# Sums of the FFN output's weights: when they are asked for, which slots they use, and no low parts kept in DRAM

## The chip, the cores and the metric

The kernel runs on one core of a Trainium2 chip. The metric is the time of one execution in microseconds of the device. Before the change the median of three runs is 929.23 us (925.81 to 930.81).

## The reference

One layer of a decoder trunk on 512 tokens of width 1024, all float32. The stages that matter here:

```python
xn = _rmsnorm(h, norm1_w)
proj = xn @ w_in
z, xbc, dt_raw, q, k, v, qi, ki, wi, u, gates = _split_proj(proj)
...
y = _ssd_scan(xh, dt, A, Bm, Cm)                      # state-space mixer, chunks of 128 tokens
y_ssd = _rmsnorm((y + d_skip * xh) * jax.nn.silu(z), ssd_norm_w)
...
merged = g[:, :, 0] * (y_ssd @ w_up_ssd) + g[:, :, 1] * (y_att @ w_up_attn) + g[:, :, 2] * (y_pool @ w_up_pool)
h = h + merged @ w_out
hn = _rmsnorm(h, norm2_w)
a_part, b_part = jnp.split(hn @ w_ffn_in, 2, axis=-1)
return h + (jax.nn.silu(a_part) * b_part) @ w_ffn_out   # followed by one more RMSNorm
```

`w_ffn_out` has 2816 rows (the hidden units) and 1024 columns. It is an input, so sums of its parts can be formed at any time before the last product.

## The kernel before

**Number format.** TensorE multiplies float32 through pairs: each operand is split into a high part (`wh`, a cast to a shorter format by ACT) and a low part (`wl`, the difference, by DVE), and a product is three matmuls, high by high, high by low and low by high. `split` and `split_w` write these pairs for weights and activations; `raw` is a weight tile as loaded.

**Order of the stages on TensorE.** Its instructions stay in the order in which the program writes them (`manual_schedule` for PE). First come the index scores, keys, queries and values and the pooling projections; then, in `gate_merge(2, ...)`, the gates and the up projection of the pooling branch, then the channels of the convolution (`xbc`, twelve tiles) and the gate `z`; then `gate_merge(1, ...)` for attention and `gate_merge(0, ...)` for the state-space branch. `gate_merge` runs a loop over `f`: `gate(f)` loads gate weights and multiplies, `up(f)` multiplies the branch's output by its up projection and merges. For branches 1 and 2, `up` lags `gate` by two steps; for branch 0 all eight gates come first (`f` 0 to 7) and the eight up products after (`f` 8 to 15). Then follow the output projection (`token_major`, PE tile `acc`), the FFN's first product (tile `r`, seven block products per unit in a Strassen scheme) and its second (tile `o`, again seven products over a scheme of 2 by 2 blocks).

**The state-space chain.** `ssd_gens` is a stream: a generator whose steps `tick` puts between matmuls of whatever stage is running, by a clock that the program keeps while it is being written. After attention it builds, for each of two groups of heads, `btok`, `cbt` and four `xdt` (six slots of tag "A") and `selp` and three `hst` (four slots of "T2"); eight pairs of heads then each need DVE and ACT to make the decay matrix `L` (`seg` on PE, a minimum on DVE, exponentials on ACT, a product with `cbt` on DVE), then PE tiles `ebc`, `yd` and `yo`. Last, `ssd_norm` takes the mean square (`ssq`), its root (`rt`, two steps on DVE and one on ACT), spreads it (`rstd`), and splits the result into `ysh` (tag "yP") and `ysl` (eight slots of "A"), which the up products of branch 0 read. The chain runs beside the gates and up products of branch 1.

**The other engines.** Instructions of DVE, ACT, POOL and SP are not held to the program's order: they are put in order ahead of time by what is ready and has a slot, earlier program text first among ready ones. On the chip each engine then takes its own list strictly in order. SBUF tiles come from tags with a fixed number of slots (`SLOTS`: "A" 12, "T2" 8, "xbc" 12, "T1" 4 and so on); a tile waits until a slot of its tag is free.

**The sums.** For the second FFN product four of the seven right-hand sides are sums of blocks of `w_ffn_out`: U1 to U4. `prestage(u)` (u = 0 to 10, 11 units) loads four blocks `wb` (tag "T2", 256 KB each, by SP, L721), adds them on DVE into four `wsum` tiles (tag "xbc"), and for the two blocks that are used unsummed (products 1 and 2) makes high parts `whigh` on ACT and low parts `wlow` on DVE, all in "xbc". POOL's queue stores the four sums and two low parts in DRAM (L732; tensors U and L). The call stands in branch 0's loop: unit `f - 1` ahead of `gate(f)` for f = 1 to 11.

**The output stage.** `OUT` lists 42 steps (p, v): product p = 1, 2, 6, 5, 7, 4, 3, six steps each, the last of a product half as large. `prepare_out(n)` runs two steps ahead: it loads the right-hand side `oraw` (a block of `w_ffn_out`, or a stored sum; L1324), casts it to `wh` on ACT, and gets its low part `wl`: for products 1 and 2 by a load of L (L1337), else by a subtraction on DVE. `sums_left` makes sums of the hidden activations on DVE (`hid`, `xsum`) in products 1 and 2, and `split_left` splits the left-hand side (`hl`). Where nearly all operations go through a helper, the profile puts them on line 90, so groups are told apart by their tiles.

Of the kernel before, what the change touches and what calls it, by code (L numbers as in the profile page):

```python
# [8 lines left out]
F32 = mybir.dt.float32  # L9
R32 = mybir.dt.float32r  # L10
# [3 lines left out]
P = 128  # L14
# [81 lines left out]
def kernel(  # L96
# [91 lines left out]
    def nm(s):  # L188
        uid[0] += 1
        return f"{s}_{uid[0]}"  # L190
# [4 lines left out]
    def slot(tag, name, dtype=F32, shape=(P, T)):  # L195
        return spool.tile(list(shape), dtype, name=nm(name), tag=tag, bufs=SLOTS[tag])
# [514 lines left out]
    def stored(name, v):  # L711
        if (name, v) not in kept:
            kept[name, v] = sums_pool.tile([P, len(members(v)), T], F32, name=f"{name}_{v}", tag=f"{name}_{v}")
        return kept[name, v]

    def prestage(u):
        b = {}
        for c in range(2):
            for n in range(2):
                b[c, n] = slot("T2", "wb")  # L720
                SP.dma_start(b[c, n], wfo[c, n][:, u, :])  # L721
        got = {}
        for name, x, y in (("U1", b[0, 0], b[0, 1]), ("U2", "U1", b[1, 1]), ("U3", b[0, 1], b[1, 1]), ("U4", "U2", b[1, 0])):
            got[name] = slot("xbc", "wsum")
            DVE.tensor_tensor(got[name], got.get(x) if isinstance(x, str) else x, y, op=OP.add)
        for name, c in (("L1", 0), ("L2", 1)):
            h = slot("xbc", "whigh", R32)
            ACT.copy(h, b[c, 0])
            got[name] = slot("xbc", "wlow")
            DVE.tensor_tensor(got[name], b[c, 0], h, op=OP.subtract)  # L730
        for name, t_ in got.items():
            nc.gpsimd.dma_start(stored(name, u // 2)[:, u % 2, :], t_)  # L732

    def gate_merge(br, w_up, nk, yh, yl, ready):
        wd = 2048 // nk
        ths, raws = {}, {}

        def gate(f):
            if f % 2 == 0:
                raws["g"] = load_cols([(win, G0 + br * D + f * P, 256)], KD)  # L740

            def evac(ps):
                if br == 0:
                    if f % 4 == 0:
                        ths[f // 4, "all"] = slot("yA", "gths", F32, (P, 4, T))
                    ths[f] = ths[f // 4, "all"][:, f % 4, :]
                else:
                    ths[f] = slot("th", "gth")
                ACT.activation(ths[f], ps, AF.Tanh, scale=0.5)

            proj_job(raws["g"][:, :, tsl(f % 2)], evac)

        def up(f):
            if (f * P) % wd == 0:
                raws["u"] = load_cols([(w_up[0], f * P, wd)], nk)
            o = (f * P) % wd

            def body(w):
                ready()
                pu = pmm("up")  # L760
                product(pu, *w, yh, yl, nk)
                th = ths[f]
                if merged[f] is None:
                    merged[f] = slot("m", "merged")
                    DVE.scalar_tensor_tensor(merged[f], th, 1.0, pu, OP.add, OP.mult)
                else:
                    DVE.scalar_tensor_tensor(th, th, 1.0, pu, OP.add, OP.mult)
                    if br == 0:
                        DVE.tensor_tensor(merged[f], merged[f], th, op=OP.add)
                        finish_merged(f)  # L770
                    else:
                        POOL.tensor_tensor(merged[f], merged[f], th, op=OP.add)

            job(lambda: split_w(raws["u"][:, :, o:o + P], (P, nk, P)), body)

        skew = SKEW if br else KD
        for f in range(KD + skew):
            if br == 0 and 1 <= f <= NU:
                prestage(f - 1)
            if f < KD:  # L780
                gate(f)
            if f >= skew:
                up(f - skew)

    def mixes_ready():
        for st in mixes:
# [226 lines left out]
            st.live[0][1] = at + NLAG  # L1013
        return st

    def token_major(w, nk, ah, al, tail, done, ahead=None, tag=None):
        acc = {}
        for t in range(NT):
            for hf in range(2):
                acc[t, hf] = pmm("acc") if t < 2 else paux("acc")  # L1020
        keep = []

        def term(t, k, wh, wl, hfs=(0, 1)):
            a, b = ah(k)[:, tsl(t)], al(k)[:, tsl(t)]
            for hf in hfs:
                cs = slice(hf * T, hf * T + T)
                PE.matmul(acc[t, hf], lhsT=a, rhs=wh[:, cs], start=(k == 0), stop=False)
                PE.matmul(acc[t, hf], lhsT=a, rhs=wl[:, cs], start=False, stop=False)
            for hf in hfs:
                cs = slice(hf * T, hf * T + T)  # L1030
                PE.matmul(acc[t, hf], lhsT=b, rhs=wh[:, cs], start=False, stop=(k == nk - 1))
            tick()

        for k in range(nk):
            if k % 2 == 0:
                raw = (slot(tag, "raw", F32, (P, 2, D)) if tag else
                       wpool.tile([P, 2, D], F32, name=nm("raw"), tag="raw", bufs=2))
                SP.dma_start(raw, w[k * P:(k + 2) * P, :].rearrange("(k p) n -> p k n", p=P))
            wh, wl = split_w(raw[:, k % 2, :], (P, D))
            if k < nk - tail:  # L1040
                for t in range(NT):
                    term(t, k, wh, wl)
            else:
                keep.append((k, wh, wl))
        if ahead is not None:
            ahead()
        for t in range(NT):
            if t < NT - 1:
                for k, wh, wl in keep:
                    term(t, k, wh, wl)  # L1050
            else:
                for hf in range(2):
                    for k, wh, wl in keep:
                        term(t, k, wh, wl, (hf,))
            done(t, acc[t, 0], acc[t, 1])
# [271 lines left out]
    def prepare_out(n):  # L1327
        if n >= len(OUT):
            return
        p, v = OUT[n]  # L1330
        w = len(members(v))
        load_right(p, v)
        h = wpool.tile([P, 2, T], R32, name=nm("wh"), tag="wh")
        l = wpool.tile([P, 2, T], R32, name=nm("wl"), tag="wl")
        ACT.copy(h[:, :w, :], oraws[p, v])
        if p in (1, 2):
            SP.dma_start(l[:, :w, :].bitcast(F32), stored(f"L{p}", v))  # L1337
        else:
            DVE.tensor_tensor(l[:, :w, :], oraws[p, v], h[:, :w, :], op=OP.subtract)
        orights[p, v] = h, l  # L1340
        split_left(p, v)
        if n + 1 < len(OUT):
            load_right(*OUT[n + 1])
# [62 lines left out]
    def close_row(t):  # L1406
# [3 lines left out]
        DVE.tensor_scalar(ys[t][:, 1, :], ys[t][:, 1, :], rs, None, OP.mult)  # L1410
        SP.dma_start(of[tsl(t), T:D], ys[t][:, 1, :])

    prepare_out(0)
    prepare_out(1)
    for n, (p, v) in enumerate(OUT):
# [58 lines left out]
```

## Time and profile before

| what | us |
|---|---|
| median of three runs | 929.23 (925.81 to 930.81) |
| the profiled execution, its own time | 924.42 |
| its span, first to last instruction | 922.7 |
| TensorE busy | 886.4 (96%) |
| VectorE busy | 683.7 (74%) |
| ScalarE busy | 458.7 (50%) |
| GpSimd busy | 144.4 (16%) |
| mean granted clock of TensorE | 0.988 |

In rows of instructions each has its line, engine, operation, `out<-in` by tile names, shape and count. In a row of waits, "A x <- B y: total, times, longest" says that engine A sat idle before its instruction on tile x until B's on y ended; "DMA U<-wsum" as the releaser is the landing of a store of a sum, which also sets its slot free. A line of the order of time starts with its start and duration, and has in brackets the idle time before it and what ended that. In the tables by stretches each engine has its busy time and, in brackets, its count of instructions; PEclk is the clock granted to TensorE, 1.00 being full speed; the last two are the busy share and the rate of the DMA engines.

### The profile page before, as it was taken

The page shows a single profiled execution, that of the slowest core. Times are in us where ns is not written, and L with a number is a line of the kernel's source. Part 1 is how long each engine was busy: PE and PEld are TensorE (multiplying, and loading weights), DVE is VectorE, ACT ScalarE, POOL GpSimd, SP SyncE. Part 2 cuts the span into 40 slices and gives each one's busy share as a digit, 9 for nine tenths or more (in the row PEclk, how much of TensorE's full clock was granted, in tenths as well). Part 3 has the DMA queues.
Part 4 walks back from the last instruction along what each step waited for, and adds up shares of the span by engine and source line. Part 5 has one row for each costly group of instructions (what it writes and reads, how often), then busy time and mean ns, then how long its engine had stood idle before and what let it go on. Part 6 is the DMA issues. An engine that isn't in the chain of part 4 may idle for free.

```text
span 922.7 us, 13363 instructions
## 1 busy us (share of the span) xinstructions
PE 886.4 (96%) x5083; PEld 765.4 (83%) x5083; DVE 683.7 (74%) x1095; ACT 458.7 (50%) x791; POOL 144.4 (16%) x165
## 2 busy tenths in 40 slices
PE   9999999999999999887998999999999999999997
PEld 7877778888888777666786887999999999977885
DVE  5588999955654467777876635999888879766786
ACT  6546433355553244453542325965455455556665
POOL 3160000001110223446542002200000000001011
PEclk9999999999999999998999999999999999999998
DMA  7222112323212112757799725123422223697553
GB/s 242 69 92 92 46 46 92 94 89 92 92 47 81 57 46 92 233 189 248 256 408 363 264 92 182 47 92 130 145 92 92 93 98 108 220 340 249 183 193 127
DMA packets 95202, 134.10 MB, mean 145 GB/s; under 512 B 6745, under 2 KB 65697, under 8 KB 95138
## 3 DMA queue, kind: packets, MB, share of 16 engines
q1 hardware_dynamic: 88178, 113.58, 37.5%
q0 software_dynamic: 5280, 17.31, 4.7%
q10 hardware_dynamic: 1680, 2.36, 0.7%
q8 instruction: 40, 0.66, 0.3%
q14 instruction: 24, 0.20, 0.1%
HBM read 111.73 MB, written 21.50 MB: 144 GB/s over the span
## 4 chain that ended last, share of the span: by engine, by line
PE 38%; DVE 6%; DMA 5%; issue 3%; ACT 2%; POOL 1%; DVEq 0%; SPq 0%; POOLq 0%; ACTq 0%
PE r L90 23%; PE o L90 9%; PE up L90 4%; DMA wb<-in_w_ffn_out_dram 4%; PE acc L90 2%; DVE wl L90 2%; DVE ms L90 1%; DVE xr L90 1%; DMA wl<-L 1%; DMA U<-wsum 1%; DMA raw<-in_w_ffn_in_dram 1%; DVE wsum L90 1%; DVE wlow L90 0%; DVE early L90 0%; ACT acc L90 0%
## 5 line engine op out<-in xcount | busy, mean ns | idle before, releaser
L90 ACT CAST wh<-raw 128x1024 fp32r<-128x1024 f32 (+1 forms) x151 | 150.9, 1003 | 174.4 <-PE r L90 59.4
L90 DVE TENSOR_TENSOR wl<-raw,wh 128x1024 fp32r<-128x1024 f32 (+1 forms) x149 | 175.4, 1178 | 70.8 <-ACT wh L90 70.5
L90 PE MATMUL mm<-xnh,wh 128*128 128x512 f32 (+1 forms) x480 | 192.7, 402 | 0.0
L90 PE MATMUL mm<-xnh,wl 128*128 128x512 f32 (+1 forms) x480 | 183.4, 382 | 1.3 <-DVE wl L90 1.3
L90 PE MATMUL mm<-xnl,wh 128*128 128x512 f32 (+1 forms) x480 | 183.2, 382 | 0.3 <-DVE xnl L90 0.3
L90 PE MATMUL r<-T,wh 128*128 128x256 f32 x704 | 127.9, 283 | 0.0
L90 PEld LDWEIGHTS r<-T,wh 128*128 128x128 f32 x704 | 109.8, 192 | 0.0
L90 PEld LDWEIGHTS mm<-xnh,wl 128*128 128x128 f32 x480 | 90.5, 189 | 19.6 <-DVE wl L90 1.7
L90 PEld LDWEIGHTS mm<-xnh,wh 128*128 128x128 f32 x480 | 91.1, 190 | 15.9 <-issue 2.0
L90 PEld LDWEIGHTS mm<-xnl,wh 128*128 128x128 f32 x480 | 90.9, 189 | 15.5 <-issue 1.4
L90 PE MATMUL r<-T,wl 128*128 128x256 f32 x352 | 99.6, 283 | 0.0
L90 PE MATMUL o<-wh,hl 128*128 128x512 f32 x308 | 95.4, 390 | 0.1
L90 PE MATMUL r<-B,wh 128*128 128x256 f32 x464 | 84.8, 283 | 0.0
L90 PEld LDWEIGHTS r<-B,wh 128*128 128x128 f32 x464 | 72.4, 192 | 0.0
L90 PEld LDWEIGHTS o<-wh,hl 128*128 128x128 f32 x308 | 57.8, 188 | 12.3 <-ACT wh L90 0.5
L90 PEld LDWEIGHTS r<-T,wl 128*128 128x128 f32 x352 | 67.6, 192 | 0.0
L90 PE MATMUL r<-B,wl 128*128 128x256 f32 x232 | 65.7, 283 | 0.0
L90 PE MATMUL o<-wl,hl 128*128 128x512 f32 x154 | 60.6, 394 | 3.2 <-DVE wl L90 1.9
L90 POOL TENSOR_TENSOR ys<-xr,fnrow 128x512 f32<-128x512 f32 x6 | 11.8, 1972 | 309.4 <-DMA oraw<-U 253.3
L90 ACT CAST wh<-oraw 128x1024 fp32r<-128x1024 f32 (+1 forms) x42 | 41.0, 978 | 23.8 <-PE o L90 15.8
L90 PEld LDWEIGHTS r<-B,wl 128*128 128x128 f32 x232 | 44.5, 192 | 0.0
L90 POOL TENSOR_TENSOR xbc<-xbc,tap 128x509 f32<-128x509 f32 x12 | 13.0, 1086 | 187.1 <-DVE xbc L90 181.2
(280 smaller groups left out, 1601.4 us busy)
## 6 DMA issues: line engine op xcount, KB each, us to landing
raw<-in_w_in_dram SPq DMA_DIRECT2D x26, 1024.0 KB, 5.0
raw<-in_w_ffn_in_dram SPq DMA_DIRECT2D x23, 1024.0 KB, 5.0
wb<-in_w_ffn_out_dram SPq DMA_DIRECT2D x44, 256.0 KB, 5.4
U<-wsum POOLq DMA_DIRECT2D x44, 256.0 KB, 5.7
oraw<-U SPq DMA_DIRECT2D x20, 512.0 KB, 3.7
oraw<-in_w_ffn_out_dram SPq DMA_DIRECT2D x15, 512.0 KB, 5.1
L<-wlow POOLq DMA_DIRECT2D x22, 256.0 KB, 5.7
wl<-L SPq DMA_DIRECT2D x10, 512.0 KB, 4.7
```

Source lines behind the costliest of these rows:

```text
L90: return fn(*args, **kw)
```

## The change

The sums move from tag "xbc" to tag "A". The high and low parts of the two unsummed blocks and their stores go. Of the four stores of a unit, U2 and U4 stay on POOL's queue, and U1 and U3 go to SP's. A unit is now asked for by `stage_next`, which does nothing until the state-space stream has put out all its steps in the program; it is called at the end of each step of branch 0's loop (every step to f = 7, then odd ones) and after each of the first five rows of weights in `token_major`. In the output stage products 1 and 2 compute their low parts on DVE as the others do. The parameter `tag` of `token_major`, which no call used, is dropped.

```diff
         for name, x, y in (("U1", b[0, 0], b[0, 1]), ("U2", "U1", b[1, 1]), ("U3", b[0, 1], b[1, 1]), ("U4", "U2", b[1, 0])):
-            got[name] = slot("xbc", "wsum")
+            got[name] = slot("A", "wsum")
             DVE.tensor_tensor(got[name], got.get(x) if isinstance(x, str) else x, y, op=OP.add)
-        for name, c in (("L1", 0), ("L2", 1)):
-            h = slot("xbc", "whigh", R32)
-            ACT.copy(h, b[c, 0])
-            got[name] = slot("xbc", "wlow")
-            DVE.tensor_tensor(got[name], b[c, 0], h, op=OP.subtract)
         for name, t_ in got.items():
-            nc.gpsimd.dma_start(stored(name, u // 2)[:, u % 2, :], t_)
+            (nc.gpsimd if name in ("U2", "U4") else SP).dma_start(stored(name, u // 2)[:, u % 2, :], t_)
+
+    staged = [0]
+
+    def stage_next():
+        if staged[0] < NU and ssd_st.done():
+            prestage(staged[0])
+            staged[0] += 1
...
         for f in range(KD + skew):
-            if br == 0 and 1 <= f <= NU:
-                prestage(f - 1)
             if f < KD:
                 gate(f)
             if f >= skew:
                 up(f - skew)
+            if br == 0 and (f < KD or f % 2):
+                stage_next()
...
             if k < nk - tail:
                 for t in range(NT):
                     term(t, k, wh, wl)
+                stage_next()
...
         ACT.copy(h[:, :w, :], oraws[p, v])
-        if p in (1, 2):
-            SP.dma_start(l[:, :w, :].bitcast(F32), stored(f"L{p}", v))
-        else:
-            DVE.tensor_tensor(l[:, :w, :], oraws[p, v], h[:, :w, :], op=OP.subtract)
+        DVE.tensor_tensor(l[:, :w, :], oraws[p, v], h[:, :w, :], op=OP.subtract)
```

More of the change, by code (lines that the diff above doesn't have):

```diff
@@ L1014, in start_now, with token_major @@
         return st
-    def token_major(w, nk, ah, al, tail, done, ahead=None, tag=None):
+    def token_major(w, nk, ah, al, tail, done, ahead=None):
         acc = {}
@@ L1035, in token_major @@
             if k % 2 == 0:
-                raw = (slot(tag, "raw", F32, (P, 2, D)) if tag else
-                       wpool.tile([P, 2, D], F32, name=nm("raw"), tag="raw", bufs=2))
+                raw = wpool.tile([P, 2, D], F32, name=nm("raw"), tag="raw", bufs=2)
                 SP.dma_start(raw, w[k * P:(k + 2) * P, :].rearrange("(k p) n -> p k n", p=P))
@@ L1411, in close_row @@
         SP.dma_start(of[tsl(t), T:D], ys[t][:, 1, :])
+    assert staged[0] == NU
     prepare_out(0)
```

## Prediction

> **What bounds the kernel now.** I read the page first, then the table of busy time by stretches, then who waited for whom on PE, DVE, ACT and SP, and last the order of time around the longest waits.
>
> ```profile
> span 922.7 us, 13363 instructions
> ## 1 busy us (share of the span) xinstructions
> PE 886.4 (96%) x5083; PEld 765.4 (83%) x5083; DVE 683.7 (74%) x1095; ACT 458.7 (50%) x791; POOL 144.4 (16%) x165
> ```
>
> TensorE is busy 96% of the span, so it is the bound, and whatever happens to another engine counts only where it makes PE idle or lowers its clock. 36 us are idle in all. The next table shows the two stretches in which the sums of the weights are made: from the end of the first four heads' pairs to the first gate of the last branch (363.9 to 441.4), and from there to the last sum.
>
> ```profile
> core 0: us, PE busy (x) PEld busy (x) DVE busy (x) ACT busy (x) POOL busy (x), PEclk, DMA share, GB/s
> 363.90:441.40 77.50, 64.71 (x323) 52.28 (x323) 57.54 (x78) 32.41 (x69) 38.87 (x44) 0.93 0.68 226
> 441.40:498.00 56.60, 51.83 (x220) 41.76 (x218) 45.28 (x66) 27.17 (x40) 27.28 (x40) 0.97 0.92 339
> ```
>
> PE idles 77.50 - 64.71 = 12.8 us in the first and 56.60 - 51.83 = 4.8 us in the second: half of all its idle time in a seventh of the span. The granted clock costs more on top: 0.07 of 64.71 is 4.5 us, 0.03 of 51.83 is 1.6 us. So 23.7 us are lost where the changed code runs. Who ended PE's waits there:
>
> ```profile
> PE yd L90 <- DVE L L90: 7.5, 3, 3.1
> PE up L90 <- DVE wl L90: 3.5, 2, 2.7
> PE ebc L90 <- ACT E L90: 2.9, 1, 2.9
> PE rstd L90 <- ACT rt L90: 2.4, 1, 2.4
> PE mm L90 <- DVE wl L90: 1.3, 1, 1.3
> ```
>
> Three of the five (yd, ebc, rstd; 12.8 us) are the state-space chain, the other two weights' low parts. None is a shortage of DVE time (57.54 of 77.50): DVE and ACT take their instructions in order, and what stands at their head waits for a transfer. DVE first, then ACT:
>
> ```profile
> DVE wsum L90 <- DMA wb<-in_w_ffn_out_dram: 11.0, 6, 2.9
> DVE wlow L90 <- DMA U<-wsum: 6.1, 3, 2.7
> DVE wsum L90 <- DMA L<-wlow: 4.2, 3, 2.8
> ```
>
> ```profile
> ACT whigh L90 <- DMA U<-wsum: 10.7, 5, 4.1
> ACT whigh L90 <- DVE wlow L90: 9.0, 3, 4.2
> ```
>
> The first row is a load that has not landed. The other DMA rows are waits for a slot: wlow, whigh and wsum share the tag "xbc" with the twelve convolved channels, and a slot comes free only when an earlier sum's store has landed.
>
> **The change part by part.** *High and low parts gone.* In each of 11 units, two casts on ACT, two subtractions on DVE and two stores by POOL go.
>
> ```profile
> L90 DVE TENSOR_TENSOR wlow<-wb,whigh x22: 677/686/693, 377.1 to 496.1; 128x512 f32<-128x512 f32 x22
> ```
>
> ```profile
> L90 DVE TENSOR_TENSOR wsum<-wsum,wb x22: 676/692/1982, 369.4 to 494.8; 128x512 f32<-128x512 f32 x22
> ```
>
> That is 22 x 0.69 = 15.1 us of DVE; 44 sums stay (22 of the second row and as many of two wb, 30 us). What matters is the waits that go with them. Here is what stood ahead of the longest one:
>
> ```profile
> 411.88 0.69 DVE L90 TENSOR_TENSOR wlow<-wb,whigh 128x512 f32<-128x512 f32 x1 [2.07 <-DMA U<-wsum]
> ...
> 416.19 0.69 DVE L90 TENSOR_TENSOR wlow<-wb,whigh 128x512 f32<-128x512 f32 x1 [1.29 <-DMA U<-wsum]
> 416.80 0.68 DVE L90 TENSOR_TENSOR L<-L,cbt 128x512 f32<-128x512 f32 x1
> ```
>
> The product L at 416.80, for which PE waits its 3.1 us, stands behind two low parts that waited 2.07 and 1.29 us and took 1.4 us; the cast whigh that waits on the first of them holds up E on ACT, PE's 2.9 us. Both are credited whole. Of the other two yd waits (7.5 - 3.1 = 4.4 us) I credit 2.8: the third of the low parts' slot waits, 6.1 - 2.07 - 1.29 = 2.7, stands ahead of the first, and mostly plain sums ahead of the second. The rstd wait:
>
> ```profile
> 433.00 0.16 DVE L90 TENSOR_SCALAR rt<-ssq 128x4 f32<-128x4 f32 x1
> 433.48 0.69 DVE L90 TENSOR_TENSOR wsum<-wsum,wb 128x512 f32<-128x512 f32 x1 [0.32 <-DVE rt L90]
> 434.09 0.17 DVE L90 RECIPROCAL rt<-rt 128x4 f32<-128x4 f32 x1
> ```
>
> A sum slips between the two steps of rt, and more of them stand ahead; half, 1.2 us, is credited. Chain: 3.1 + 2.9 + 2.8 + 1.2 = 10.0 of 12.8 us, and the same share of the clock's 4.5, 3.5. In the second stretch:
>
> ```profile
> 486.12 0.69 DVE L90 TENSOR_TENSOR wsum<-wsum,wb 128x512 f32<-128x512 f32 x1 [2.79 <-DMA L<-wlow]
> ...
> 488.54 1.22 DVE L90 TENSOR_TENSOR wl<-raw,wh 128x1024 fp32r<-128x1024 f32 x1
> ```
>
> This slot wait is followed by the wl for which PE waits 2.7 us; it goes with the stores of L: 2.7, and 2.7/4.8 of 1.6 = 0.9 of clock. The 1.3 and the other 0.8 stay. Credit in all: 10.0 + 3.5 + 2.7 + 0.9 = 17.1 us.
>
> The clock term has a rule against it. The rows show 0.93 and 0.97 though no single wait of PE there is over 3.1 us. The Trainium skill, "TensorE: Matmul & The Clock Gate", Part 1, says that the clock is halved after an idle window of about 3.4 us; by that rule these waits would cost no clock and the credit would be 12.7, the time 923.1. The trace disagrees: the rows decide, and the rule gets no chance of its own.
>
> *Asked for later, in other slots.* The text asks for unit 0 after the first gate of the last branch, at about 441 in PE's order, but its loads are issued long before that:
>
> ```profile
> 360.40 0.34 SPq L721 DMA_DIRECT2D wb<-in_w_ffn_out_dram  x1
> ```
>
> Apart from PE's, instructions are put in order by what is ready and has a slot. SP shows which slot:
>
> ```profile
> SPq L721 <- DVE wsum L90: 38.4, 10, 5.9
> SPq L721 <- DVE wlow L90: 37.8, 15, 8.6
> ...
> SPq L721 <- PE ebc L90: 11.3, 2, 10.1
> ```
>
> The loads' "T2" slots come free with ebc and yo of the fourth pair; this isn't changed. At the same place btok, cbt and four xdt of the first group leave "A", six slots, where "xbc" had few. So my likeliest case is that sums still run ahead into the chain, and, no longer held by slots, faster: two or three units more before 441. Waits for loads are 11.0 us over 11 units, 1.0 each: 2.5 us new on the path. For slots of "A" I take one wait of the size seen, 2.1 us, bounds 0 and the old 6.1 + 4.2 = 10.3. New waits: 4.6 us.
>
> *Two of four stores on SP.* Each waits for its sum, and SP's loads behind it wait too. SP waits for wsum and wlow already (38.4 + 37.8 us), so I take nothing; the end of this cost is a rival below. POOL keeps half of its issues, and nothing on PE's path waits there.
>
> *Twelve subtractions come back in the output stage,* in place of twelve loads of L.
>
> ```profile
> L90 DVE TENSOR_TENSOR wl<-oraw,wh x30: 680/1221/2319, 837.7 to 911.6; 128x1024 fp32r<-128x1024 f32 x25, 128x512 fp32r<-128x512 f32 x5
> ```
>
> ```profile
> 805.70:820.60 14.90, 14.90 (x68) 12.13 (x67) 9.77 (x18) 9.10 (x13) 0.00 (x0) 1.00 0.94 353
> 820.60:837.00 16.40, 15.28 (x68) 12.31 (x66) 7.43 (x13) 8.52 (x12) 0.00 (x0) 1.00 0.95 325
> ```
>
> The rows are product 1 and product 2, six steps each. The steps prepare two ahead, so product 1 gets five whole and one half: 5 x 1.22 + 0.69 = 6.8, and DVE would need 9.77 + 6.8 = 16.6 in PE's 14.9: 1.7 us late. Product 2 gets 3 x 1.22 + 0.69 = 4.4: 11.8 of 16.4, covered. Two more (2.4 us) fall before 805.7. PE's 16.40 - 15.28 = 1.1 us of waiting there is for a low part's load and goes. I take +2.0, with bounds -1.1 (all hidden) and +11.1 (the ten in the stage all exposed; the rows' surplus of 1.7 speaks for the low end).
>
> Sum: -17.1 + 4.6 + 2.0 = -10.5 us. The profiled execution took 924.4 us (922.7 of span), so it would be 913.9; it lies 4.8 under the median of the three runs, 929.2, and the forecast is set against that: **918.7 us**.
>
> **The rivals.** *The sums wait until the chain is over,* as the text has it. For it: the eight ysl also want "A". Against: ysl is written only from 443.8 on, and six slots stand open from 363.9.
>
> ```profile
> L90 DVE TENSOR_TENSOR ysl<-xbc,ysh x8: 679/688/691, 443.8 to 471.9; 128x512 fp32r<-128x512 f32 x8
> ```
>
>  In this case the whole first loss goes, and if the later units hide under the 90 us of gates and up products that follow, the second too: -12.8 - 4.5 - 4.8 - 1.6 + 2.0 = -21.7, or 907.5.
>
> *The waits change their name.* From 443.8 on ysl comes to hold eight of twelve "A" slots to the end of the up products, so one unit's four sums fill the rest and the next wait for stores to land; loads still come late. If "A" brings back all the old slot waits (10.3 in place of 2.1, +8.2) the sum is -2.3: 926.9, no change that can be told. Against it: nobody needs four of these at once for whigh and wlow any more.
>
> *SP becomes the wait.* A store at SP's head waits for DVE, and the raw weights of the up products and the output projection stand behind it.
>
> ```profile
> L90 DVE SCALAR_TENSOR_TENSOR gths<-gths,up x8: 681/685/689, 498.9 to 535.9; 128x512 f32<-128x512 f32 x8
> ```
>
> ```profile
> 497.90 0.38 SPq L219 DMA_DIRECT2D raw<-in_w_up_ssd_dram  x1
> ```
>
> ```profile
> DMA to landing us min/median/max: 5.0/7.5/10.0
> ```
>
> The up products end 5.3 us apart, so the fifth begins at 498.9 + 3 x 5.3 = 514.8. Its raw, issued at 497.90, lands at 505.4; with 1.2 for its low part (the 1.22 above) and, as an estimate, as much for the cast, 7.0 us are spare. SP's longest wait for such a result is 8.6. From a wait of 7.0 on, PE idles: at 8.6 plus a second store's 0.7 us sum, 2.3 us for each of the eight raws, 18.4 us; -10.5 + 18.4 = +7.9, 937.1, slower. For it: the Trainium skill, "DMA: Bandwidth & Descriptors", Anatomy of one DMA, says that a DMA's semaphore wait is taken by the issuing sequencer before dispatch; the SP rows agree. Against: SP carries such waits already, and none of PE's five is for raw.
>
> **How the numbers follow.** 0.5% is 4.6 us, about what can be told from no change here. Chances: the forecast 0.54, its own range 912 to 925; waiting for the chain's end 0.20; waits renamed 0.15; SP 0.11. The first two are faster: 0.74; then 0.15 and 0.11. The range takes the second case's time with 2 us below it and, above, the renamed waits with about 2 us of the output bound: 905.5 to 929.
>
> **What would show it.** Right: in the chain's stretch PE's waits for L, E and rt fall from 12.8 to about 5 us with the clock near 0.98; no wait of DVE or ACT on a store of U or L; sums running before the chain's last yd; DVE over 90% busy in product 1, PE idle there 1 to 3 us. Wrong: waits of DVE for stores of U as long as before (renamed); PE waiting for a raw, with SP's row for L721 and the stores above 8 us (SP); PE idle over 5 us in product 1; or the first sum only after rstd, with no PE wait on L (the second case).

## The result and the profile after

The changed kernel takes 907.23 us (median of 4 runs, 905.85 to 908.09) where the kernel before, on the same chip, takes 929.15 (925.81 to 930.81). The ratio is 0.977 (95% interval 0.974 to 0.980). The profiled execution took 906.6 us against 924.42, 17.8 less; its span is 904.9 against 922.7. The medians lie 21.9 apart, more than the profiles, because the profiled execution of before lay 4.8 under its median and this one only 0.6 under its own. The forecast was 10.5 less. One execution of a run below, a_ACT, took 1445 us at a granted clock of 0.56; that run's median here is that of its other three.

The page's first part, after:

```profile
span 904.9 us, 13215 instructions
## 1 busy us (share of the span) xinstructions
PE 879.8 (97%) x5083; PEld 762.5 (84%) x5083; DVE 681.7 (75%) x1085; ACT 446.3 (49%) x769; POOL 115.6 (13%) x121
```

PE's idle time fell from 36.3 to 25.1 us, and its busy time by 6.6 us though it runs the same 5083 instructions: the mean granted clock went from 0.988 to 0.995. To see where, we follow one group of matmuls in each stage. The rows give min/median/max in ns and then the first and the last start. Before:

```profile
L90 PE MATMUL rstd<-ident,rt x8: 275/275/376, 434.9 to 435.8; 128*128 128x128 f32 x8
L90 PE MATMUL up<-ysh,wl x64: 389/389/628, 489.8 to 535.5; 128*128 128x512 f32 x64
L90 PE MATMUL acc<-wh,mgl x64: 387/389/397, 536.6 to 581.6; 128*128 128x512 f32 x64
L90 PE MATMUL o<-wh,hl x308: 387/389/501, 805.7 to 915.4; 128*128 128x512 f32 x154
```

After:

```profile
L90 PE MATMUL rstd<-ident,rt x8: 271/276/276, 420.1 to 420.9; 128*128 128x128 f32 x8
L90 PE MATMUL up<-ysh,wl x64: 389/389/505, 472.6 to 515.8; 128*128 128x512 f32 x64
L90 PE MATMUL acc<-wh,mgl x64: 387/389/629, 516.9 to 567.7; 128*128 128x512 f32 x64
L90 PE MATMUL o<-wh,hl x308: 387/389/397, 792.2 to 897.5; 128*128 128x512 f32 x154
```

Read down the columns, this is the ledger. The state-space chain reaches rstd 14.8 us sooner (434.9 to 420.1). From there to the last up product another 4.9 are gained (19.7 in all). The output projection then gives 5.8 back (from 46.1 us, 581.6 - 535.5, to 51.9). From its end to the first matmul of the output stage nothing moves (224.1 and 224.5). The output stage takes 105.3 in place of 109.7, 4.4 less. -14.8 - 4.9 + 5.8 + 0.4 - 4.4 = -17.9, within rounding what the two profiles differ by.

The table by stretches, after. The first two are the clock times that the prediction used; the stages in them lie up to 20 us earlier than before the change. The third holds most of the output projection and the start of the FFN's first product, the fourth is product 1:

```profile
363.90:441.40 77.50, 74.68 (x392) 61.27 (x391) 56.22 (x73) 38.45 (x75) 24.12 (x18) 1.00 0.39 124
441.40:498.00 56.60, 54.84 (x241) 44.70 (x240) 34.59 (x46) 15.78 (x20) 6.71 (x12) 1.00 0.88 300
536.00:588.00 52.00, 47.61 (x284) 41.84 (x283) 41.59 (x65) 37.00 (x81) 13.44 (x12) 0.93 0.52 179
792.20:807.20 15.00, 15.00 (x68) 12.42 (x67) 14.96 (x25) 9.73 (x14) 0.00 (x0) 1.00 0.66 219
```

In the first stretch PE idles 2.8 us where it idled 12.8, at full clock where it had 0.93, and the DMA share fell from 0.68 to 0.39: hardly anything of the sums runs there any more. What PE still waits for in the whole run, of the changed part:

```profile
PE yd L90 <- DVE L L90: 4.2, 3, 1.4
PE acc L90 <- DVE wl L90: 3.8, 1, 3.8
...
PE mm L90 <- DVE wl L90: 1.8, 1, 1.8
```

The waits for E, for rt, for the up products' low parts and those of the output stage are gone; a new one of 3.8 us stands in the output projection. Of the 4.2 us for L, 2.8 fall in the first stretch, where it was 7.5; the other 1.4 stand ahead of it, as they did before the change. Why the chain is free, two groups show, the last step of the split of the chain's result and the first step of the sums:

```profile
L90 DVE TENSOR_TENSOR ysl<-xbc,ysh x8: 675/678/1773, 425.4 to 439.7; 128x512 fp32r<-128x512 f32 x8
```

```profile
L90 DVE TENSOR_TENSOR wsum<-wb,wb x22: 678/686/694, 440.3 to 550.8; 128x512 f32<-128x512 f32 x22
L721 SPq DMA_DIRECT2D wb<-in_w_ffn_out_dram x44: 328/442/1217, 360.8 to 543.8; - x44
```

The loads still begin at 360.8, as foretold. But the first sum starts at 440.3, straight behind the last ysl at 439.7, not at 367. What DVE's sums wait for now:

```profile
DVE wsum L90 <- DMA wb<-in_w_ffn_out_dram: 23.4, 11, 5.3
...
DVE wsum L90 <- DMA U<-wsum: 6.9, 4, 3.2
```

These are waits at DVE's head of 30.3 us, more than before, and PE feels little of them: most lie beside gates and up products whose pairs are already made.

### The profile page after: what moved, and what is told of

Read it like the earlier page. It is cut to its first block, busy times and chain, and to the rows that moved or that the text cites. A ratio compares the mean times of both kernels' runs of the same rounds, so it can differ in the third digit from the quotient of the medians.

```text
span 904.9 us, 13215 instructions
## 1 busy us (share of the span) xinstructions
PE 879.8 (97%) x5083; PEld 762.5 (84%) x5083; DVE 681.7 (75%) x1085; ACT 446.3 (49%) x769; POOL 115.6 (13%) x121
## 4 chain that ended last, share of the span: by engine, by line
PE 76%; DVE 12%; DMA 5%; issue 2%; ACT 2%; POOL 1%; SPq 1%; DVEq 0%; ACTq 0%; POOLq 0%
PE mm L90 25%; PE r L90 24%; PE o L90 10%; PE up L90 7%; DVE wl L90 3%; DMA wb<-in_w_ffn_out_dram 3%; PE acc L90 2%; PE yatt L90 2%; DMA U<-wsum 2%; DVE work L90 1%; DVE top L90 1%; PE ptr L90 1%; PE yd L90 1%; PE logit L90 1%; DMA raw<-in_w_out_dram 1%
## 5 line engine op out<-in xcount | busy, mean ns | idle before, releaser
L90 PEld LDWEIGHTS r<-T,wh 128*128 128x128 f32 x704 | 109.8, 192 | 0.0
L90 PEld LDWEIGHTS mm<-xnl,wh 128*128 128x128 f32 x480 | 90.7, 189 | 15.7 <-issue 1.4
L90 PEld LDWEIGHTS mm<-xnh,wh 128*128 128x128 f32 x480 | 90.5, 189 | 15.6 <-issue 1.6
L90 PEld LDWEIGHTS o<-wh,hl 128*128 128x128 f32 x308 | 57.8, 188 | 11.9
L90 DVE TENSOR_TENSOR wl<-oraw,wh 128x1024 fp32r<-128x1024 f32 (+1 forms) x42 | 48.8, 1167 | 6.6 <-ACT wh L90 6.3
```

Of the source, the lines that this page charges most:

```text
L90: return fn(*args, **kw)
```

## The experiments

Theory: ysl, asked for earlier in the text, has the first claim on the slots of "A", so no sum gets one until the chain is over; asking late keeps the sums behind the ysl also afterwards; absent low parts shorten the queue and the output stage; stores on SP cost nothing. Rivals: one part alone does it (fewer instructions, or the later asking), or the slots do not matter.

Each run has its median, its ratio to the kernel before run beside it, and for its profiled execution the start of rstd and of the last up, acc and o matmul, as in the ledger above (before: 434.9, 535.5, 581.6, 915.4; after: 420.1, 515.8, 567.7, 897.5).

| run | us | ratio (95%) | rstd | up | acc | o |
|---|---|---|---|---|---|---|
| b_A | 935.23 | 1.006 (1.003 to 1.008) | 420.3 | 545.2 | 591.2 | 927.4 |
| b_noL | 916.48 | 0.985 (0.983 to 0.988) | 436.3 | 531.2 | 577.2 | 906.6 |
| b_late | 943.05 | 1.016 (1.012 to 1.020) | 434.5 | 530.3 | 595.7 | 933.0 |
| a_xbc | 921.07 | 0.990 (0.987 to 0.993) | 432.1 | 525.4 | 579.8 | 910.8 |
| a_early | 923.10 | 0.994 (0.991 to 0.996) | 418.0 | 538.3 | 584.4 | 914.1 |
| a_L | 927.26 | 0.999 (0.997 to 1.001) | 418.8 | 515.1 | 583.3 | 917.0 |
| a_ysl | 915.17 | 0.985 (0.980 to 0.991) | 425.7 | 520.6 | 577.4 | 906.7 |
| a_POOL | 920.14 | 0.993 (0.991 to 0.995) | 420.6 | 525.4 | 580.4 | 910.3 |

**One part alone, added to the kernel before.** First the slots:

```diff
-            got[name] = slot("xbc", "wsum")
+            got[name] = slot("A", "wsum")
```

> Before, with one part of the change: the sums take slots of tag A in place of xbc; high and low parts, stores and the place of asking stay. Theory S (the slots keep the sums out of the chain: ysl was asked for earlier from the same tag, so no sum gets a slot until ysl has them): first sum after rstd, PE idle in the chain's stretch down by 8 to 12 us, time 915 to 921, output stage as before. Theory X (the low parts and their slot waits were the loss) and theory L (asking later is what counts): 927 to 931, sums still from about 368 on.

The chain is freed by this line alone: rstd at 420.3. But by the end of the up products the kernel is 9.7 us later than before, and its time lies above all that was expected. PE's waits from 363 to 600, b_A:

```profile
PE mm L90 <- DVE wl L90: 9.0, 2, 4.5
PE up L90 <- ACT ysh L90: 8.0, 2, 4.4
...
PE up L90 <- DVE wl L90: 2.7, 1, 2.7
```

DVE's order of time in b_A shows what these low parts stood behind:

```profile
457.79 0.69 DVE L90 TENSOR_TENSOR wlow<-wb,whigh 128x512 f32<-128x512 f32 x1
458.39 1.22 DVE L90 TENSOR_TENSOR wl<-raw,wh 128x1024 fp32r<-128x1024 f32 x1
466.93 0.69 DVE L90 TENSOR_TENSOR wsum<-wb,wb 128x512 f32<-128x512 f32 x1 [7.33 <-DMA wb<-in_w_ffn_out_dram]
```

A sum waits 7.33 us for its load; that sum, three more and two low parts, with 4.5 us from 466.93 on, stand ahead of the next wl at 471.39. Asked for while the chain is still putting out its steps, the sums get their slots between the ysl: the last ysl starts at 504.6 in b_A, at 439.7 in the changed kernel, and the up products wait for it and for its high part.

Then the low parts alone, left out of the sums and of the loads in the output stage:

```diff
-        for name, c in (("L1", 0), ("L2", 1)):
...
-        if p in (1, 2):
-            SP.dma_start(l[:, :w, :].bitcast(F32), stored(f"L{p}", v))
-        else:
-            DVE.tensor_tensor(l[:, :w, :], oraws[p, v], h[:, :w, :], op=OP.subtract)
+        DVE.tensor_tensor(l[:, :w, :], oraws[p, v], h[:, :w, :], op=OP.subtract)
```

> Before, with one part of the change: no high and low parts and no stores of L; products 1 and 2 of the output stage subtract on DVE. Sums stay in xbc and are asked for early. Theory X: the chain's waits go with the low parts, 8 to 10 us, and the output stage gains the 4.4 us that it gained in the changed kernel: 914 to 917. Theory S: sums still stand in the chain and run ahead faster, so PE's waits for L and E fall by a third at most: 919 to 923, of which 4.4 us is the output stage. Theory L: only the output stage, 924 to 926.

This is the only part that gains by itself: 1.5%. Sums run from 366 on, and PE still waits for the chain (yd 11.1 us, rstd 3.3): rstd comes 1.4 us later than before. In the stretch from 363.9 to 441.4 PE is idle for 14.4 us, where it was 12.8 before the change, at a lower clock, and in the next stretch not at all:

```profile
363.90:441.40 77.50, 63.10 (x303) 50.84 (x302) 56.88 (x78) 27.01 (x58) 38.40 (x44) 0.89 0.75 247
441.40:498.00 56.60, 56.60 (x251) 46.86 (x250) 36.52 (x47) 21.67 (x29) 12.10 (x19) 1.00 0.78 278
```

The gain lies behind the chain: 4.3 us by the last up, and 4.4 more in the output stage, which takes 105.3 us as in the changed kernel. The time is the one that theory X named, but not for X's reason: the chain's waits did not go. Where a low part stood ahead of a product L before, another sum stands now:

```profile
416.35 0.69 DVE L90 TENSOR_TENSOR wsum<-wb,wb 128x512 f32<-128x512 f32 x1 [3.80 <-DMA wb<-in_w_ffn_out_dram]
416.96 0.68 DVE L90 TENSOR_TENSOR L<-L,cbt 128x512 f32<-128x512 f32 x1
```

Then the later asking alone (`stage_next` and its two calls, in place of the call ahead of `gate(f)`):

> Before, with one part of the change: units are asked for by the test on the state-space stream, later in the text; slots, low parts and stores stay. Theory L: first sum after rstd, 914 to 918. Theories S and X: the sums still start at about 368, because xbc has free slots and nothing earlier waits for them; the last units move into the output projection, and the time is 929 to 936, no faster.

Slower by 1.6%, more than any theory had it. The slots of "xbc" let the sums start at 366.9, the chain is not freed (434.5), and the last sums now run to 592.8, into the output projection, which takes 65.4 us in place of 46.1: PE waits 6.5 us for the rows of the next norm and 5.9 for a high part.

**One part taken out of the changed kernel.** Slots back to "xbc" (`got[name] = slot("xbc", "wsum")`):

> The changed kernel with the sums put back in xbc, all else changed. Theory S: the sums stand in the chain again (first at 365 to 375), PE idles there 7 us or more, 913 to 920. Theories L and X: 906 to 909, first sum after 435.

Sums start at 367.8, rstd at 432.1: 12.0 us of the chain's gain are gone, and 13.8 of the time, a little more than theory S had.

Asked for early again (the call ahead of `gate(f)` in place of `stage_next`):

> The changed kernel with units asked for as before the change (unit f - 1 ahead of gate f), so that asking is no longer held back until the state-space stream is done; slots, stores and the missing low parts stay changed. Theory S1 (the slots take the sums out of the chain, and asking late adds nothing there but pushes the last units into the output projection): rstd at about 420 as in the changed kernel, the 3.8 us wait and low clock in the output projection gone, 901 to 904. Theory S2 (asking late also keeps the sums behind ysl; asked early they get slots of A in between and ysl and the gates' low parts stand behind their loads, as where only the slots were changed): rstd at about 420, but 5 us or more of PE idle between rstd and the first up product, 909 to 918.

The chain stays free (418.0), but the up products end 22.5 us later than in the changed kernel, and the time is above both theories' ranges. PE's waits, a_early:

```profile
PE mm L90 <- ACT wh L90: 9.8, 1, 9.8
PE up L90 <- ACT wh L90: 8.6, 2, 5.1
```

As in b_A, sums stand between the ysl (the last at 458.0 here, 439.7 in the changed kernel), and gate weights are loaded late: ACT's cast of one waits 12.50 us for its raw. So slots and asking do different work: the slots clear the chain up to rstd, the asking clears the stretch from rstd to the up products.

Low parts back (both stored by POOL and loaded in the output stage):

> The changed kernel with high and low parts and their stores and loads back (in xbc as before; L1 and L2 on POOL's queue). Theory that the slots did the most: rstd at about 420; the output stage loses the 4.4 us and the rest of the sums' stretch 2 to 6: 913 to 918. Theory X (the low parts were the loss): 922 to 930.

All of the change's gain is gone, 20.0 us, as theory X had it, though chain and up products are as early as in the changed kernel (418.8, 515.1). The output projection takes 68.2 us, and the output stage 109.8 again:

```profile
PE tr L90 <- ACT rows L90: 7.2, 1, 7.2
PE acc L90 <- ACT wh L90: 6.4, 1, 6.4
PE acc L90 <- DVE wl L90: 3.5, 2, 2.8
```

With six tiles a unit the sums take until 565.4 in place of 551.4, and PE waits for the rows of the next norm and for the output projection's weights.

The slot theory itself: the sums stay in "A" and all is as in the changed kernel, but ysl goes to "xbc":

```diff
-l = slot("A", "ysl", R32)
+l = slot("xbc", "ysl", R32)
```

> The changed kernel with ysl in tag xbc in place of A; the sums stay in A, and every other part of the change stays. Theory S (it is ysl, asked for earlier from the same tag, that keeps the sums waiting): the sums run into the chain again, first at 365 to 375, PE waits for L 7 us or more, 914 to 922. If tag A by itself or the later asking kept them out: 906 to 909, first sum after 435.

```profile
L90 DVE TENSOR_TENSOR wsum<-wb,wb x22: 678/685/1780, 366.0 to 555.8; 128x512 f32<-128x512 f32 x22
```

With nothing of the chain's in line for "A" the sums run from 366.0, 74 us sooner, in the same slots, asked for at the same place; rstd comes at 425.7, 5.6 us later. PE's waits in the chain are 8.5 us (6.1 for L, less than the 7 that was foretold, and 2.4 for rt) where the changed kernel has 2.8. So it is the queue for a tag that holds the sums back: its slots go out in the order in which the text asks, though the earlier one may be written 60 us later. The last yd starts at 408.6 in the changed kernel; what holds the sums from there to 440, slots or only the later place in the text, these runs do not separate. The up products end 4.8 us later than in the changed kernel; as much again is lost in the output projection, where PE waits 7.1 us for one low part.

**The stores.** The prediction took two stores on SP at nothing. All four on POOL, else the changed kernel:

```diff
-            (nc.gpsimd if name in ("U2", "U4") else SP).dma_start(stored(name, u // 2)[:, u % 2, :], t_)
+            nc.gpsimd.dma_start(stored(name, u // 2)[:, u % 2, :], t_)
```

> The changed kernel with all four stores of a unit on POOL's queue, as before the change. If SP's waits for the sums held back its loads: the DVE's waits for wb fall by 5 us or more and the time by 2 to 5, to 902 to 905. If half of the stores on SP costs nothing or helps: 906 to 911.

Slower than expected by far: 920.14, so SP's two stores are worth 12.9 us. Between 440 and 560, DVE's sums wait 15.7 us for stores (9 times) where they waited 6.9 (4 times), and 12.0 for loads where they waited 23.4. Two theories: SP's stores hold its loads back, or POOL's queue frees the slots later. Four runs were made to tell them apart. All four on SP, then two on ACT's queue, then two on SP without the rest of the change:

> The changed kernel with all four stores of a unit on SP. With all four on POOL it took 920.1, with two on each 907.2. Theory "SP's stores hold its loads back" (a store at SP's head waits for its sum, so the next units' loads go out one by one and do not crowd the stores and the raw weights): all four hold them at least as well, 903 to 909, and the raw of the up products lands in 5.5 to 6.5 us as in the changed kernel (6.0; 10.4 with the stores on POOL). Theory "POOL's queue is slow" (its stores land in 4.6 and 5.5 us, SP's in 3.8, and a slot comes free that much later): also 902 to 907, with DVE's waits for stores below 5 us. Rival "two queues share the work" (neither may carry all four): 912 to 922, with raws of the up products issued late and PE waiting over 5 us for wl.

> The changed kernel with U1 and U3 stored by ACT's queue in place of SP's; U2 and U4 stay on POOL. The queue is of the same kind as SP's, but SP's loads are not held back. Theory "SP's stores hold its loads back": SP's loads run ahead as with all stores on POOL, the raw of the up products lands in 9 to 11 us, and the time is 914 to 922. Theory "POOL's queue is slow": half the stores land fast, as in the changed kernel: 905 to 911, DVE's waits for stores 5 to 9 us. On top of either, 22 issues on ACT cost it some 0.3 to 0.6 us each and wait in order for DVE: up to 3 us more on PE.

> The kernel before without low parts, and with U1 and U3 stored by SP; sums stay in xbc, asked for as before. Without the SP stores it took 916.5. If SP's stores help wherever sums run: 905 to 912, with fewer or shorter waits for yd and rstd than 14.4 us. If they help only where all sums run beside the up products and the output projection (four slots of A left, raws of 1 MB behind them): 914 to 919. If SP's waits for sums delay what the chain's stretch loads: above 919.

All on SP took 903.98 (0.974, 0.971 to 0.977), as both theories had it, but the raw landed in 8.0 us, not 6; DVE's waits for stores were 3.9 us, as the second had it. Two on ACT's queue took 915.70 (0.986, 0.982 to 0.991). That fits the holding by its time and not by its mark (raw landed in 4.9); DVE's waits for stores, 12.6 us, fit the slow queue no better, though ACT's stores landed in 4.5 us and POOL's in 5.6. And the run has its own reason to be slow: ACT takes its list in order and waited 18.2 us ahead of high parts (wh) and as much ahead of gths for the sums that it was to store. It does not decide. In the kernel before without low parts, SP's stores change nothing that can be told (915.12 against 916.48; ratios 0.985 and 0.985); the sums run in "xbc" from 368 to 481, and DVE's waits for stores are 7.0 us with SP's stores and 0.6 without, though SP's land in 3.1 us there and POOL's in 4.9. So a store that lands sooner does not pay everywhere.

The one that separates most has POOL carry all sums, and SP wait for U1 and U3 all the same, by a second, tiny store:

```diff
+            nc.gpsimd.dma_start(stored(name, u // 2)[:, u % 2, :], t_)
+            if name in ("U1", "U3"):
+                SP.dma_start(sums_pool.tile([1, 16], F32, ...), t_[0:1, :16])
```

It ran beside the changed kernel and the one with all four on SP:

> The changed kernel itself, on the same chip as the two that follow: 905.5 to 908.5 by every theory.

> All four stores on SP once more, beside the changed kernel on one chip. Theory "SP's stores hold its loads back": 2 to 4 us below the changed kernel (904.0 against 907.2 so far). Rival "no difference": within 1 us of it.

> All four stores on POOL, as in the run that took 920.1, and for U1 and U3 a second, tiny store of 16 elements on SP, so that SP waits for these sums as in the changed kernel while the sums themselves go by POOL's queue. Theory "SP's stores hold its loads back": 904 to 911, DVE's waits for stores of U at most 8 us (15.7 with POOL alone, 6.9 in the changed kernel). Theory "POOL's queue is slow": 917 to 922, these waits 12 us or more. Third, "the order of DVE's list": the holding, known to the order that is made ahead of time, puts fewer sums ahead of the last low parts before the up products (in DVE's order 3, 7, 13, 16, 19, 20, 24 sums precede the first seven low parts in the changed kernel, 3, 7, 13, 18, 23, 24 and 24 with POOL alone); the tiny stores restore this in part, so 908 to 915 with PE's wait for wl between the two.

The changed kernel took 907.07, all on SP 903.70, the tiny stores 919.14 (0.990, 0.986 to 0.993). Holding SP does not help (it waits 66.7 us at the tiny stores, 57.8 at the changed kernel's); that SP carries the sums does. DVE's waits between 440 and 560, a_mark, and the landing of its stores (KB each, median us from issue to landing):

```profile
DVE wsum L90 <- DMA wb<-in_w_ffn_out_dram: 18.5, 10, 5.0
DVE wsum L90 <- DMA U<-wsum: 14.7, 9, 4.3
```

```profile
U<-wsum POOLq DMA_DIRECT2D x44, 256.0 KB, 5.2
```

The same of a_SP2:

```profile
DVE wsum L90 <- DMA wb<-in_w_ffn_out_dram: 10.0, 6, 4.0
...
DVE wsum L90 <- DMA U<-wsum: 2.3, 2, 1.8
```

```profile
U<-wsum SPq DMA_DIRECT2D x44, 256.0 KB, 3.7
```

And the changed kernel, half and half:

```profile
U<-wsum SPq DMA_DIRECT2D x22, 256.0 KB, 3.8
U<-wsum POOLq DMA_DIRECT2D x22, 256.0 KB, 4.6
```

A sum's slot is held 1.5 us longer when POOL stores it (5.2 against 3.7); ysl has eight of the twelve slots, so a late landing can hold DVE, and what stands behind it on DVE comes late: PE waits 9.6 us for wl in a_mark from 363 to 600 (up 4.2, acc 3.0, mm 2.4), 5.6 in the changed kernel (3.8 and 1.8), and in a_SP2 not at all. It also waits 5.1 us for one high part of the output projection in a_mark, and 5.3 for the rows of the next norm in a_SP2. But how long DVE waits is not the whole of it: its sums wait 33.2 us in all between 440 and 560 in a_mark and 33.0 in the changed kernel (30.0 with the stores on POOL alone, 16.5 in a_SP2), so what counts is what stands behind each wait. And DVE's list differs from run to run. In a_mark it is close to the changed kernel's (the fifth and sixth low part ahead of the up products stand behind 20 and 24 sums in place of 19 and 20); in a_SP2 the first seven stand behind 3, 7, 9, 13, 16, 17 and 20. So that the queue of the stores is worth 12 us is shown; that it is worth them by slots that come free sooner, and not by the list that was made for it, is not.

All four on SP is the best version found, 3.4 us under the changed kernel beside it; its ratio of 0.974 (0.970 to 0.978) and the changed kernel's of 0.977 (0.974 to 0.980) overlap, so the step is likely and not proven.

**Tries to win back the output projection's 5.8 us.** A unit at every step of the loop, so that the last sums end sooner (`if br == 0:`); the loads in "xbc" (`b[c, n] = slot("xbc", "wb")`), with a unit at every step and without; and the loads in "xbc", the sums in "T2", each sum put behind the last ysl by hand:

> The changed kernel with a unit asked for at every step of the state-space branch's loop, also the even ones from 8 on, so that the last units come in the up products and not in the output projection. If the 3.8 us wait in the output projection comes from the last units' loads: it goes, with its clock 4 to 6 us, 901 to 904. If the crowding only moves into the up products: 906 to 910, with PE waits for wl there.

> The changed kernel with the loads wb in tag xbc (twelve slots that stand free after the chain) in place of T2, whose slots mgl takes in the up products, and a unit asked for at every step of the loop. If what is left of the loss comes from loads that wait for T2: DVE's waits for wb fall from 23 us below 8, PE's waits for wl and in the output projection go, 899 to 903. If it comes from the four slots of A that ysl leaves: waits for stores of U grow, 905 to 912.

> The changed kernel with the loads wb in tag xbc in place of T2, units asked for as in the changed kernel (odd steps from 8 on, then in the output projection). The residual's rows ask for xbc ahead of the units in the output projection and leave them two slots. If loads are the rest of the loss: 900 to 905; if the two slots hold the last units back: 908 to 914, with PE waiting in the output projection.

> The changed kernel with wb in xbc, the sums in T2 (eight slots), a unit asked for at every step, and the sums queued on DVE behind the last ysl by an order of issue in place of by the slots of A. If keeping the sums behind ysl is all that A did: rstd at about 420 as in the changed kernel, no waits for stores of U, 898 to 903. If A's scarcity also paces the sums usefully: PE waits for wl in the gates after ysl, 906 to 912.

They took 914.40, 922.41, 924.11 and 914.28 us (ratios 0.985, 0.995, 0.998, 0.988), all slower than the changed kernel. None of the times is in a range that was expected. In the first the sums end at 532.4, but the output projection still takes 53.4 us (51.9 in the changed kernel), now with a wait of 4.6 us for gths, and the up products end 7.6 us later, at 523.4: more sums ahead of them is the same loss at another place. Loads in "xbc" raise DVE's waits for stores (13.1 us in a_wbx, with 11.0 of PE on low parts of the up products) or for loads (27.1 in a_wbx_odd, whose last sums come at 579.0 and where PE waits 14.2 us once, ahead of the FFN's first product). In a_hold rstd comes at 419.3 without ysl's claim on the slots, which shows again that only the order behind ysl counts for the chain; its up products end at 525.9.

## Why the prediction was wrong

**What bounds the kernel: right.** PE, and the waits of the chain behind sums and low parts. The second stretch's 3.6 us (2.7 + 0.9) came as 4.9 from rstd to the last up product, and b_noL, where PE has no idle time left there, shows that the low parts are the reason.

**The chain's credit: right in size, by luck.** Of the chain's 12.8 us of idle time 10.0 were credited to the low parts, and 12.8 - 2.8 = 10.0 went, the clock with it (4.5 us where 3.5 were credited). But with the low parts alone gone PE is idle 14.4 us in that stretch (b_noL): other sums, and their waits for loads, take the place of the low parts ahead of L and rt. With the low parts still there and only the slots changed, rstd comes at 420.3 (b_A). The 10.0 us went because the sums left the chain, which the forecast's own case said they would not do.

**The step that failed: "So my likeliest case is that sums still run ahead into the chain".** Its 4.6 us of new waits (2.5 for loads, 2.1 for slots) never came on PE's path: the first sum starts at 440.3. The argument was that six slots of "A" stand open from 363.9 while ysl is written only from 443.8 on. It took a slot for free because nothing is written in it. a_ysl shows the mistake: a slot is spoken for by the text that asks first, and ysl is asked for ahead of every sum. The second case, "the sums wait until the chain is over", which got 0.20, is what happened, and its sign, named ahead ("the first sum only after rstd, with no PE wait on L"), is what the profile shows, but for 2.8 us of waits on L in that stretch, none over 1.4. How the forecast's case would have gone, a_ysl shows: there the sums do run ahead in "A", PE waits 8.5 us in the chain where the forecast had 12.8 - 10.0 + 4.6 = 7.4, and the time is 915.17, inside the forecast's own range.

**Its 907.5 was met by luck.** It had 17.3 us for the chain and its clock, where rstd came 14.8 sooner, and 6.4 behind it, where 4.9 came. It had no loss in the output projection, where 5.8 us were lost, and 2.0 of loss in the output stage, where 4.4 were gained. In all it had 21.7, and the two profiles differ by 17.8; that the medians differ by 21.9 comes from the profiled execution of before, which lay 4.8 us under its median.

**The output projection was not in the sum.** The last units are asked for while it runs. DVE and PE in order of time, after:

```profile
548.43 0.69 DVE L90 TENSOR_TENSOR wsum<-wb,wb 128x512 f32<-128x512 f32 x1 [2.43 <-DMA wb<-in_w_ffn_out_dram]
549.04 1.22 DVE L90 TENSOR_TENSOR wl<-raw,wh 128x1024 fp32r<-128x1024 f32 x1
...
550.31 0.79 PE L90 MATMUL acc<-wl,mgh 128*128 128x512 f32 x1 [3.77 <-DVE wl L90]
```

A low part stands behind a sum that waits for its load, the very pattern that was read in the chain, moved some 130 us on. In the stretch from 536 to 588 PE idles 4.4 us where it idled 0.4, at a clock of 0.93 where it was 1.00; the row of before:

```profile
536.00:588.00 52.00, 51.58 (x261) 43.44 (x259) 30.03 (x43) 28.62 (x61) 10.51 (x8) 1.00 0.38 132
```

**The output stage: wrong sign.** +2.0 was taken, -1.1 was the lower bound, and -4.4 came. DVE was 14.96 us busy in the 15.00 of product 1, for which 16.6 were worked out, but PE was busy for all 15.00: DVE at its limit in one product did not make PE late. The steps are prepared two ahead, and DVE had the start of the stage ready (the first low part at 787.9, the first product at 792.2). What went is more than the one wait of 1.1 us that was credited:

```profile
L90 DVE TENSOR_TENSOR wl<-oraw,wh x42: 677/1220/2318, 787.9 to 893.6; 128x1024 fp32r<-128x1024 f32 x35, 128x512 fp32r<-128x512 f32 x7
```

All 42 low parts are made on DVE, the first at 787.9, ahead of the stage; PE has no wait for them in any row, where it had 1.9 us for wl besides the 1.1 for the load. b_noL and a_L show the 4.4 us with this part alone, added and taken out (105.3 and 109.8); 3.0 of them are these waits, and the rest is not in any row of waits.

**SP's stores: not a cost but a gain.** They were taken at nothing, with 18.4 us against the change as a rival. SP waits 57.8 us for sums at these stores, and yet ACT, which casts the up products' raw weights, waits for none of them, where it waited 15.6 us before. (The rival's price rested on a landing of 7.5 us and on eight loads; the profile of before has four loads of 1 MB for these products, which landed in 10.0.) SP's stores bring 12.9 us against POOL's, which is more than the whole forecast; by which way, the runs leave open, as said above. The Trainium skill, "DMA: Bandwidth & Descriptors", SWDGE vs HWDGE vs iDMA, says that a transfer issued from GpSimd has its descriptors written by software, one from SP by hardware with a faster set-up. The trace agrees in the direction, 5.2 us to the landing from POOL's queue against 3.7 from SP's.

**What the parts are worth together.** Alone, slots cost 0.6%, later asking costs 1.6%, and no low parts gain 1.5%. Taken out of the whole, each of the four parts costs 13 to 20 us (a_POOL 12.9, a_xbc 13.8, a_early 15.9, a_L 20.0). These sum to 62.6 us for a change of 21.9, so the parts do not add: in the rows above, a wait that one part removes comes back at another place when one of the others is missing. The prediction added the parts.

## What to carry to other kernels

Before you call a slot free, look up who else asks for its tag and in which order the text asks; a tile that is written late can keep out one that is ready early, and this can be used on purpose to hold background work behind a critical chain. Background work on an in-order engine wants its loads landed, its slots free, and a place in the order behind what TensorE waits for; one of the three alone moves the wait and does not remove it. When a change has several parts, price them in the order of time, each after the one before it, and ask at the end of every stretch what the moved work now stands in front of.

## What the runs showed of the hardware

A 256 KB store of a sum lands in 3.7 us (median) from SP's queue in a_SP2 and in 5.2 from POOL's in a_mark, where one queue carries all 44. In the changed kernel, where they share, it is 3.8 and 4.6, and 4.4 and 4.7 in the second profile of the same kernel (a_again). In all eleven runs that split the stores between SP and POOL, SP's landed sooner, by 0.1 to 1.8 us. It is no fixed price: in b_late all 44 went by POOL's queue, spread over 226 us in place of some 120, and landed in 3.6.

And the clock: behind the one wait of 3.77 us after the change, the granted clock is 0.53 from 548 to 552 and 0.62 from 552 to 556, with 1.00 on both sides. This agrees with the Trainium skill, "TensorE: Matmul & The Clock Gate", Part 1, by which it takes some 3.4 us of idle time. But before the change two waits of 2.89 and 3.07 us, with PE at work for 0.8 us between them, were followed by 0.51 from 416 to 420 and 0.63 from 420 to 424; and after it, with no wait over 1.4, the chain's stretch has 1.00.
